# Second tile's gated outputs in the normed input's place, and the last queries' transposes tied into the second gate projection

## The chip, the cores and the metric

The kernel runs on one core of one Trainium2 chip. The metric is the device time of one execution in microseconds. Three runs of the kernel before gave 296.37 us as the median (296.13 to 296.43). A core has a matrix engine (PE, with its weight loads as PEld), three engines for element-wise work (DVE, ACT, POOL) and a sync engine (SP) that issues the DMAs. PE writes only to PSUM, which has eight banks; DVE and ACT read them out.

## What is computed

Two layers on 256 tokens of width 1024, in float32. Each layer is `x = x + rms_norm(mixer(rms_norm(x)))`. Layer 0's mixer is gated linear attention and isn't touched. Layer 1's is sparse attention with 16 heads in 4 groups:

```python
p = (h @ w_in)                       # queries, six key/value parts, gate logits, gate path z
q = rope(q, positions) * DH ** -0.5
...                                  # compressed, selected and windowed attention, per group
o = einsum('bshc,bshcd->bshd', gates, out).reshape(B, S, NSA_Q) * silu(z)
return o @ w_out
```

## The kernel before

The 256 tokens are two tiles t of 128. Every large product is made of three float32r matmuls (high by high, high by low, low by high half: `mm3`, L211 to L213), so each weight and each activation is split: ACT makes the high half (L190), DVE or POOL the low one (L196).

The stretch that the change touches begins once layer 1's keys and values are there. Its parts, in the order in which the program names them (L1209 to L1235):

- Query projections Q(p, t) for half p of the heads and tile t (`q_steps`). Each ends with the rotary embedding: two DVE products and a POOL sum (L827), which leaves the rotated queries in `qr`.
- Query transposes QT(p, t) (`q_T`): four PE transposes (L982) into one PSUM bank of the tag "t", then two ACT copies (L987) and two DVE subtractions (L988) into a tile of the tag "qS".
- Gate projections Z0 and Z1 (`z_steps`): 96 matmuls each, eight steps k of twelve, which read the normed input `hT` and fill the two "acc" banks. At the end DVE and ACT make the gate `zT` from them (L362, L372, L373).
- Units U(g, t), one for each group g and tile t. `scores` makes four heads of scores (L1020) in the three "s" banks; DVE masks them and takes the minimum (L1025), ACT takes the exponential (L1027), POOL weighs the result (L1061). `values` transposes the weighed scores into "t" banks, four transposes a round (L1091), copies each round out by ACT or DVE in turn (L1095, L1097), and multiplies with the values (L1105); one transpose for the compressed part (L1111) and the products of it (L1129) end it. A unit of tile 0 has two rounds, one of tile 1 four. There are two "t" banks.
- `finish` multiplies a unit's output with the gate (L356) and splits it (L357, L358) into `ofT[t]`, the gated outputs. These are four tiles (two tokens' tiles, high and low) of the tag "qS", which has six buffers that hold the queries too.
- Output projections O0 and O1 (`out_steps`): 48 matmuls each, into the "acc" banks.

So the order is: Q(0,1), U(0,0), QT(0,1), Z0, U(1,0), Q(1,0), the gated outputs of U(0,0) and U(1,0), QT(1,0), Q(1,1), U(2,0), QT(1,1), Z1, U(3,0), their gated outputs, the loads and splits of the output weights, O0, the four units of tile 1, O1.

A planner turns this into one fixed queue for each engine: among the instructions that are ready by its estimated times it takes the one named first. What it may pass is limited by `chain`, which holds the projections' matmuls among themselves in program order, by `after` (behind a given instruction in the queue, without a semaphore), and by `paced`: the splits of the output weights are tied to steps of Z1 (L1230; 2 of 8 halves of the first 512 columns and 2 of 8 of the second to steps 2 and 3, the others to steps 4 to 7). The raw weights have four buffers.

Of the kernel before, what the change touches and what calls it, by code (L numbers as in the profile page):

```python
# [10 lines left out]
F32R = mybir.dt.float32r  # L11
# [5 lines left out]
P = 128  # L17
D = 1024
S = 256
NT = S // P  # L20
KT = D // P
# [66 lines left out]
def hybrid_kernel(ctx: ExitStack, tc: tile.TileContext, x, positions, pre_norm, post_norm,  # L88
# [3 lines left out]
    nc = tc.nc  # L92
    base = ctx.enter_context(tc.tile_pool(name="base", bufs=1))
# [4 lines left out]
    def nm(s):  # L98
        _n[0] += 1
        return f"{s}_{_n[0]}"  # L100

    def bank(tag="t"):
        return ps.tile([P, 512], F32, tag=tag, name=nm(tag), bufs=BANKS[tag])

    def f(ap):
        return ap.bitcast(F32)

    def after(ins, prev):

        if prev is not None:  # L110
            tc.add_manual_dep(ins.ins, prev.ins.name, mybir.DependencyInfo(
                mybir.DependencyClass.NoSync, mybir.DependencyReason.DATA), reason="issue order")
        return ins
# [10 lines left out]
    def dma(dst, src):  # L124
        queue[0] = after(nc.sync.dma_start(dst, src), queue[0])
# [5 lines left out]
    lp = l1.enter_context(tc.tile_pool(name="l1", bufs=1))  # L131
    C1 = lp.tile([P, C_L1 - C_L0], F32, tag="c1", name="c1")

    def cc(name):
        o, w = COFF[name]
        t, at = (C0, 0) if o < C_L0 else (C1, C_L0) if o < C_L1 else (C2, C_L1)
        return t[:, o - at:o - at + w]
# [10 lines left out]
    ident = cc("ident")  # L148
# [61 lines left out]
    def mm3(o, a, b, start, stop, **kw):  # L210
        m = nc.tensor.matmul(o, a[0], b[0], start=start, stop=False, **kw)  # L211
        nc.tensor.matmul(o, a[0], b[1], start=False, stop=False, **kw)  # L212
        return m, nc.tensor.matmul(o, a[1], b[0], start=False, stop=stop, **kw)  # L213
# [3 lines left out]
    def chain(first, final):  # L217

        after(first, last[0])
        last[0] = final  # L220
# [42 lines left out]
    def residual(t, o, gb):  # L263

        ss = base.tile([P, 8], F32, tag="ss", name=nm("ss"), bufs=4)
        yg = [base.tile([P, H], F32, tag="xg", name=nm("yg"), bufs=2) for _ in range(2)]

        def done(n):
            nc.scalar.activation(yg[n], o[n], AF.Square, accum_out=ss[:, n:n + 1])  # L269
            if n == 0:  # L270
                nc.vector.tensor_scalar(ss[:, 2:3], ss[:, 0:1], D * EPS, None, op0=ALU.add)
            else:

                nc.vector.tensor_add(ss[:, 4:5], ss[:, 1:2], ss[:, 2:3])
                nc.gpsimd.tensor_tensor(ss[:, 3:4], ss[:, 4:5], half[:, :1], op=ALU.pow)
            nc.vector.scalar_tensor_tensor(yg[n], o[n], float(D ** 0.5), gb[:, n * H:(n + 1) * H], op0=ALU.mult,  # L276
                                           op1=ALU.mult)
            if n == 1:
                for m in range(2):
                    xx = X[:, t, m * H:(m + 1) * H]  # L280
                    nc.vector.scalar_tensor_tensor(xx, yg[m], ss[:, 3:4], xx, op0=ALU.mult, op1=ALU.add)
        return done
# [77 lines left out]
    def gate_of(o, dst):  # L360

        nc.vector.tensor_tensor(dst, o.rearrange("p (j n) -> p j n", j=2), rb.unsqueeze(1).to_broadcast([P, 2, S]),  # L362
                                op=ALU.mult)
        th = base.tile([P, 2, S], F32, tag="xg", name=nm("th"), bufs=2)
        silu2(dst, dst, th)
# [196 lines left out]
    w, n = wraw[:RANK + 1], RANK + 1  # L562
# [24 lines left out]
    b = bank()  # L587
# [44 lines left out]
    for t in range(NT):  # L632
# [3 lines left out]
        for hp in range(2):  # L636
            b = bank()
# [7 lines left out]
        if t == 0:  # L645
            b = bank()
# [17 lines left out]
        b = bank()  # L664
# [21 lines left out]
    ch_z = [Chunk(w_in, G_Z, 512).load(homes=homes)]  # L686
# [7 lines left out]
    for t in range(NT):  # L694
        aT = aTs[t]
        ob = []
        for hp in range(2):
            b = bank("s")
            for hh in range(2):
                h = 2 * hp + hh  # L700
# [5 lines left out]
        if t == 0:  # L706
            Ssb = [lp.tile([P, GH, GDV], F32R, tag=a, name=nm("S")) for a in ("q", "k")]
            for hp in range(2):
                b = bank("s")
                for hh in range(2):  # L710
                    h = 2 * hp + hh
# [15 lines left out]
    for c in range(2):  # L727
# [4 lines left out]
        for t in range(NT):  # L732
            b = bank()
# [52 lines left out]
    lp = ctx.enter_context(tc.tile_pool(name="l2", bufs=1))  # L786
# [106 lines left out]
    ch_z = [Chunk(w_in, N_Z + p * 512, 512) for p in range(2)]  # L893
# [43 lines left out]
    def pe(m):  # L937
        return m

    def run(steps, n=99):  # L940
        for _ in range(n):
            if next(steps, None) is None:
                break
# [8 lines left out]
                done(o)  # L952
            yield 1

    def proj_T_steps(chunk, done):
        o = [bank("acc") for _ in range(2)]
        for k in range(KT):
            for j in range(4):
                a, b = mm3(o[j // 2][:, (j % 2) * S:(j % 2 + 1) * S], chunk.part(k, j * P, (j + 1) * P),
                           [h[:, k, :] for h in hT], k == 0 and j % 2 == 0, k == KT - 1, skip_group_check=True)  # L960
                chunk.mm.setdefault(2 * k, a)
                chunk.mm[2 * k + 1] = a
                chain(a, b)
            if k == KT - 1:
                done(o)
            yield 1

    qS, qr = {}, {}

    def q_steps(p, t):  # L970

# [5 lines left out]
    def q_T(p, t):  # L977

        b = bank()
        r = qr[p, t]  # L980
        for m in range(4):
            pe(nc.tensor.transpose(b[:, m * P:(m + 1) * P], r[:, 2 * m:2 * m + 2].rearrange("p h d -> p (h d)"), ident))  # L982
        q = lp.tile([P, 2, 4, P], F32R, tag="qS", name=nm("qS"), bufs=6)
        bv = b.rearrange("p (m n) -> p m n", m=4)
        h = (slice(0, 64), slice(64, 128))
        for a in range(2):
            nc.scalar.activation(q[h[a], a], bv[h[a]], AF.Copy)  # L987
            nc.vector.tensor_sub(q[h[1 - a], a], bv[h[a]], f(q[h[a], a]))  # L988
        qS[p, t] = q

    def z_steps(p):
        def done(o):
            for j in range(2):
                gate_of(o[j], zT[:, p * 4 + j * 2:p * 4 + j * 2 + 2, :])
        return proj_T_steps(ch_z[p], done)

    def small(n, tag):
        return ap_.tile([P, n], F32, tag=tag, name=nm(tag), bufs=2)
# [150 lines left out]
    def out_steps(t, before=None):  # L1149

        o = [bank("acc") for _ in range(2)]
        steps = [(k, n) for k in range(6) for n in range(2)] + [(k, n) for n in range(2) for k in range(6, KT)]
        done = residual(t, o, gpost)
        for k, n in steps:
            a, b = mm3(o[n], [h[:, k, :] for h in ofT[t]], ch_o[n].part(k), k == 0, k == KT - 1)
            if before and (k, n) == (LATE, 0):
                after(a, before())
            chain(a, b)
            if k == KT - 1:
                done(n)  # L1160
            yield 1
        for n in range(2):
            sl = slice(n * H, n * H + H)
            dma(out[0, t * P:(t + 1) * P, sl], X[:, t, sl])
# [7 lines left out]
    b = bank()  # L1172
# [8 lines left out]
    b = bank()  # L1181
# [9 lines left out]
    for p in range(2):  # L1191
        for G in range(2):
# [3 lines left out]
                                    cc("blk")[rows].unsqueeze(2).to_broadcast([64, 4, DH]), op=ALU.mult)  # L1196
    run(q00)
    q_T(0, 0)
    l2a.close()
    ap_ = ctx.enter_context(tc.tile_pool(name="l2b", bufs=1))  # L1200
    ofT = [[lp.tile([P, KT, P], F32R, tag="qS", name=nm("ofT"), bufs=6) for n in "hl"] for t in range(NT)]
    ch_o = [Chunk(nsa_w_out[0], c * 512, 512) for c in range(2)]
    U = {(g, t): Unit(g, t) for g in range(GROUPS) for t in range(NT)}

    def unit(g, t):
        run(U[g, t].scores())
        run(U[g, t].values())

    ch_z[0].load().split((ch_q[0], 8))  # L1209
    run(q_steps(0, 1))  # L1210
    unit(0, 0)
    q_T(0, 1)
    run(z_steps(0))
    ch_q[1].load().split((ch_z[0], 0))
    unit(1, 0)
    run(q_steps(1, 0))
    for g in range(2):
        U[g, 0].finish()
    q_T(1, 0)
    ch_z[1].load().split((ch_q[1], 0))  # L1220
    run(q_steps(1, 1))
    unit(2, 0)
    q_T(1, 1)
    run(z_steps(1))
    unit(3, 0)
    for g in range(2, 4):
        U[g, 0].finish()
    for k in (0, 2, 4, 6):
        for n in range(2):
            ch_o[n].load(k, k + 2).split((ch_z[1], k + 2 * n + PA[12]))  # L1230
    run(out_steps(0))
    for g in range(GROUPS):
        unit(g, 1)
        U[g, 1].finish()
# [31 lines left out]
```

## Time and profile before

| what | value |
|---|---|
| median of three runs | 296.37 us (296.13 to 296.43) |
| the profiled execution | 296.34 us |
| its span, first to last instruction | 294.3 us |
| busy: PE, PEld, DVE, ACT, POOL | 281.9, 238.1, 203.9, 178.5, 178.7 us |
| mean granted TensorE clock | 0.993 |

What lies between the span and the execution's time is 296.34 - 294.3 = 2.04 us. A busy time is the sum over an engine's instructions; PE's matmuls overlap, so their busy time hides waits, and their starts tell more. The chain of waits follows the last instruction back to what released it. In the timeline a row is start, length, engine, line, operation, result and operand, count, and in square brackets an idle time before it with what ended it.

### The profile page before, as it was taken

How to read it: one execution, taken by the hardware profiler on the slowest of the kernel's cores; microseconds unless marked ns; L12 is line 12 of the kernel's file. 1: busy time of each engine (PE TensorE's matmuls, PEld its weight loads, DVE VectorE, ACT ScalarE, POOL GpSimd, SP SyncE). 2: the span in 40 equal slices, each digit the busy share in tenths (PEclk: the TensorE clock that was granted, in tenths of full speed). 3: DMA queues.
4: the chain of work that ended last, by engine and by line, in shares of the span. 5: the costliest groups of instructions: out<-in, count | busy, mean ns of one | idle time of the engine just before them, and what ended most of it. 6: DMA issues, size and time to landing. Idle time of an engine off the chain costs nothing.

```text
span 294.3 us, 5427 instructions
## 1 busy us (share of the span) xinstructions
PE 281.9 (96%) x1836; PEld 238.1 (81%) x1836; DVE 203.9 (69%) x515; ACT 178.5 (61%) x464; POOL 178.7 (61%) x207
## 2 busy tenths in 40 slices
PE   8999999999999999889999999999999899999991
PEld 7888999999999887668898789986889667678560
DVE  1779668854989968577469668797539976585323
ACT  4896788676665665545427436486278797565311
POOL 1496968985376033823539194569799779366400
PEclk9999999999999999999999999999999999999997
DMA  7997589114667255189897475704353000010001
GB/s 213 403 399 208 146 247 292 39 67 145 213 206 224 74 145 143 28 198 358 266 377 220 145 209 155 211 1 155 132 149 136 4 0 2 0 72 2 0 0 71
DMA packets 28300, 44.56 MB, mean 151 GB/s; under 512 B 2865, under 2 KB 12513, under 8 KB 28274
## 3 DMA queue, kind: packets, MB, share of 16 engines
q1 hardware_dynamic: 28242, 44.23, 47.7%
q8 instruction: 14, 0.23, 0.3%
q14 instruction: 12, 0.10, 0.1%
q10 hardware_dynamic: 32, 0.01, 0.0%
HBM read 43.18 MB, written 1.05 MB: 150 GB/s over the span
## 4 chain that ended last, share of the span: by engine, by line
PE 75%; DVE 8%; issue 7%; POOL 4%; ACT 3%; DMA 1%; SPq 0%; DVEq 0%; POOLq 0%; ACTq 0%
PE acc L213 13%; PE acc L212 13%; PE acc L211 13%; PE s L211 4%; PE s L212 4%; PE s L213 4%; PE s L468 4%; PE o L1105 4%; PE s L1020 3%; PE t L1091 3%; PE o L904 2%; DVE lo L196 2%; DMA raw<-in_gla_w_in_dram 1%; PE o L1129 1%; POOL lo L196 1%
## 5 line engine op out<-in xcount | busy, mean ns | idle before, releaser
L196 POOL TENSOR_TENSOR lo<-raw,hi 128x512 fp32r<-128x512 f32 (+2 forms) x63 | 83.6, 1350 | 41.8 <-ACT hi L190 41.8
L190 ACT ACTIVATE hi<-raw 128x512 fp32r<-128x512 f32 (+2 forms) x120 | 62.7, 581 | 17.7 <-DMA raw<-in_nsa_w_in_dram 6.1
L196 DVE TENSOR_TENSOR lo<-raw,hi 128x512 fp32r<-128x512 f32 (+2 forms) x57 | 56.1, 1006 | 11.2 <-ACT hi L190 11.0
L212 PE MATMUL acc<-hT,hi 128*128 128x256 f32 x160 | 45.0, 282 | 0.0
L211 PE MATMUL acc<-hT,hi 128*128 128x256 f32 x160 | 45.0, 281 | 0.0
L213 PE MATMUL acc<-hT,lo 128*128 128x256 f32 x160 | 44.5, 281 | 0.0
L1061 POOL TENSOR_SCALAR P<-P,cf,gates 128x128 f32<-128x128 f32 (+1 forms) x64 | 33.9, 545 | 14.2 <-DVE cf L1057 9.2
L213 PE MATMUL acc<-hi,hT 128*128 128x512 f32 (+2 forms) x104 | 36.0, 346 | 0.8 <-DVE hT L311 0.8
L211 PE MATMUL acc<-hi,hT 128*128 128x512 f32 (+2 forms) x104 | 35.8, 345 | 0.8 <-DVE yg L276 0.7
L212 PE MATMUL acc<-lo,hT 128*128 128x512 f32 (+2 forms) x104 | 35.5, 341 | 0.0
L1027 ACT ACTIVATE P<-P,mn 128x128 f32<-128x128 f32 (+1 forms) x64 | 28.4, 445 | 9.3 <-DVE mn L1025 8.9
L212 PEld LDWEIGHTS acc<-hT,hi 128*128 128x128 f32 x160 | 30.1, 188 | 0.3
L211 PEld LDWEIGHTS acc<-hT,hi 128*128 128x128 f32 x160 | 30.0, 188 | 0.1
L213 PEld LDWEIGHTS acc<-hT,lo 128*128 128x128 f32 x160 | 29.8, 188 | 0.0
L1025 DVE CUSTOM_DVE_ANT_0 P<-s,c 128x128 f32<-128x128 f32 (+1 forms) x64 | 20.8, 350 | 5.7 <-PE s L1020 3.5
L211 PEld LDWEIGHTS acc<-hi,hT 128*128 128x128 f32 x104 | 19.6, 188 | 3.7 <-ACT yg L269 1.2
L213 PEld LDWEIGHTS acc<-hi,hT 128*128 128x128 f32 x104 | 19.6, 188 | 3.3 <-DVE hT L311 1.7
L212 PEld LDWEIGHTS acc<-lo,hT 128*128 128x128 f32 x104 | 19.6, 188 | 1.8
L1091 PE MATMUL t<-c,P 128*128 128x128 f32 x96 | 17.6, 287 | 0.7 <-POOL P L1061 0.3
L440 POOL TENSOR_TENSOR lo<-raw,hi 128x512 fp32r<-128x512 f32 (+1 forms) x9 | 12.3, 1388 | 9.7 <-ACT hi L436 9.6
L1091 PEld LDWEIGHTS t<-c,P 128*128 128x128 f32 x96 | 10.8, 140 | 6.6 <-issue 3.1
L1020 PE MATMUL s<-kTh,qS 128*128 128x272 f32 (+1 forms) x48 | 14.5, 316 | 0.1
(271 smaller groups left out, 668.1 us busy)
## 6 DMA issues: line engine op xcount, KB each, us to landing
raw<-in_nsa_w_in_dram SPq DMA_DIRECT2D x24, 512.0 KB, 4.4
raw<-in_gla_w_in_dram SPq DMA_DIRECT2D x12, 512.0 KB, 5.5
raw<-in_gla_w_out_dram SPq DMA_DIRECT2D x8, 512.0 KB, 4.3
raw<-in_nsa_w_out_dram SPq DMA_DIRECT2D x8, 512.0 KB, 4.2
raw<-in_nsa_w_in_dram SPq DMA_DIRECT2D x8, 280.0 KB, 6.1
raw<-in_gla_w_in_dram SPq DMA_DIRECT2D x6, 344.0 KB, 3.4
home<-in_gla_w_in_dram SPq DMA_DIRECT2D x4, 512.0 KB, 6.7
w<-in_nsa_ck_w_dram SPq DMA_DIRECT2D x4, 512.0 KB, 7.4
```

Source lines behind the costliest of these rows:

```text
L190: m = after(nc.scalar.activation(hi[:, j, :n], raw[:, j, :n], AF.Copy), prev)
L196: eng.tensor_sub(lo[:, j, :n], raw[:, j, :n], f(hi[:, j, :n]))
L211: m = nc.tensor.matmul(o, a[0], b[0], start=start, stop=False, **kw)
L212: nc.tensor.matmul(o, a[0], b[1], start=False, stop=False, **kw)
L213: return m, nc.tensor.matmul(o, a[1], b[0], start=False, stop=stop, **kw)
L440: line(e, eng.tensor_sub(lo[:, j, :n], raw[:, j, :n], f(hi[:, j, :n])))
L468: m = nc.tensor.matmul(o[t][:, :chunk.n], hT[i][:, k, t * P:(t + 1) * P], w[j], start=(k == b == 0), stop=(k == KT - 1 and b == 2))
L1020: pe(nc.tensor.matmul(o, q[i], k[:, g, c0:c1], start=(m == 0), stop=(m == 1)))
L1025: nc.vector.tensor_tensor_reduce(out=o, in0=src, in1=masks[br], op0=ALU.add, op1=ALU.min, scale=-0.125, scalar=3.0e38, accum_out=self.mn[: ...
L1027: nc.scalar.activation(o, o, AF.Exp, scale=-1.0, bias=self.mn[:, j:j + 1], accum_out=self.sm[:, j:j + 1])
L1061: nc.gpsimd.tensor_scalar(o, o, cf[:, i * 2 + br:i * 2 + br + 1], gates[:, t, 4 * g + 2 * h + i, br + 1:br + 2], op0=ALU.mult, op1=ALU.mult)
L1091: pe(nc.tensor.transpose(b[:, i * P:(i + 1) * P], self.Pt[i][:, c0:c0 + P], ident))
```

## The change

The gated outputs of tile 1 get a place of their own: one tile of the tag "hTh", the buffer of the normed input's high half, cut in two for the high and low halves. It is named after O0, and the input is last read by Z1. The gated outputs of tile 0 stay among the "qS" buffers. And Z1 gets two ties: its first matmul of step 1 stands behind the last transpose of QT(1,0), that of step 4 behind the last of QT(1,1).

```diff
-    def proj_T_steps(chunk, done):
+    def proj_T_steps(chunk, done, behind={}):
...
                 chunk.mm[2 * k + 1] = a
+                if j == 0:
+                    after(a, behind.get(k))
                 chain(a, b)
...
-    qS, qr = {}, {}
+    qS, qr, qt = {}, {}, {}
...
-            pe(nc.tensor.transpose(b[:, m * P:(m + 1) * P], r[:, 2 * m:2 * m + 2].rearrange("p h d -> p (h d)"), ident))
+            qt[p, t] = nc.tensor.transpose(b[:, m * P:(m + 1) * P], r[:, 2 * m:2 * m + 2].rearrange("p h d -> p (h d)"),
+                                           ident)
...
-    def z_steps(p):
+    def z_steps(p, behind={}):
...
-        return proj_T_steps(ch_z[p], done)
+        return proj_T_steps(ch_z[p], done, behind)
...
-    ofT = [[lp.tile([P, KT, P], F32R, tag="qS", name=nm("ofT"), bufs=6) for n in "hl"] for t in range(NT)]
+
+    ofT = [[lp.tile([P, KT, P], F32R, tag="qS", name=nm("ofT"), bufs=6) for n in "hl"]]
...
-    run(z_steps(1))
+
+    run(z_steps(1, {1: qt[1, 0], 4: qt[1, 1]}))
...
     run(out_steps(0))
+    both_of = base.tile([P, KT, S], F32R, tag="hTh", name="ofT1")
+    ofT.append([both_of[:, :, :P], both_of[:, :, P:]])
```

## Rows read from the trace of the kernel before

**Rows 1.** The chain of waits, shares of the span by engine.
```profile
PE 75%; DVE 8%; issue 7%; POOL 4%; ACT 3%; DMA 1%; SPq 0%; DVEq 0%; POOLq 0%; ACTq 0%
```
**Rows 2.** Windows: stretch, length, busy (count) of PE, PEld, DVE, ACT, POOL; clock, DMA.
```profile
218.00:223.70 5.70, 5.70 (x51) 5.70 (x50) 4.53 (x6) 4.78 (x10) 5.70 (x6) 1.00 0.86 263
223.70:230.30 6.60, 6.60 (x36) 5.57 (x35) 6.60 (x26) 5.83 (x22) 4.95 (x4) 1.00 0.03 11
230.30:245.60 15.30, 13.72 (x91) 9.72 (x90) 13.03 (x78) 13.31 (x51) 12.60 (x30) 1.00 0.01 2
245.60:262.40 16.80, 16.54 (x105) 11.79 (x104) 11.21 (x47) 10.31 (x35) 10.71 (x19) 1.00 0.08 32
...
288.10:294.30 6.20, 0.00 (x0) 0.00 (x0) 2.31 (x5) 0.69 (x2) 0.55 (x1) 0.66 0.22 85
```
**Rows 3.** PE by form, 230.3 to 245.6 us: count, busy, mean ns, idle before.
```profile
L1020 PE MATMUL s<-kTh,qS 128*128 128x272 f32 (+1 forms) x18 | 5.8, 334 | 0.1
L1091 PE MATMUL t<-c,P 128*128 128x128 f32 x24 | 5.4, 300 | 0.6 <-POOL P L1061 0.3
...
L1129 PE MATMUL o<-pcT,vblk 64*128 64x128 f32 x8 | 1.4, 297 | 0.0
L1105 PE MATMUL o<-pT,vs_sb 128*64 128x256 f32 x8 | 1.3, 404 | 0.6 <-ACT pT L1095 0.6
```
**Rows 4.** The chain of waits after 240 us: start, length, what, count.
```profile
255.80 0.58 PE o L1105 x4
...
256.97 0.64 PE o L1129 x4
257.61 0.59 PE t L1091 x4
258.19 0.73 PE s L1020 x6
```
**Rows 5.** Timeline of POOL: the rotary sum of Q(1,1), and low halves of weights.
```profile
210.36 1.29 POOL L827 TENSOR_TENSOR rt<-rt,rt 128x512 f32<-128x512 f32 x1 [1.69 <-PE t L1091]
211.61 7.99 POOL L196 TENSOR_TENSOR lo<-raw,hi 128x512 fp32r<-128x512 f32 x6
```
**Rows 6.** Timeline of PE: query transposes, Z1's first and last matmul, U(2,0)'s first.
```profile
202.02 0.66 PE L982 MATMUL t<-c,rt 128*128 128x128 f32 x4
...
208.66 0.28 PE L211 MATMUL acc<-hT,hi 128*128 128x256 f32 x1
...
214.33 0.66 PE L982 MATMUL t<-c,rt 128*128 128x128 f32 x4
...
222.84 0.29 PE L1020 MATMUL s<-kTh,qS 128*128 128x272 f32 x1
...
223.57 0.28 PE L213 MATMUL acc<-hT,lo 128*128 128x256 f32 x1
...
236.86 0.60 PE L982 MATMUL t<-c,rt 128*128 128x128 f32 x4
```
**Rows 7.** Timeline of DVE: a gate product, a round's copy, and last query subtractions.
```profile
194.47 0.82 DVE L373 SCALAR_TENSOR_TENSOR zT<-th,zT 128x512 f32<-128x512 f32 x1
...
196.40 0.67 DVE L1097 COPY pT<-t 128x512 f32<-128x512 f32 x1
...
205.58 0.69 DVE L988 TENSOR_TENSOR qS<-t,qS 64x512 fp32r<-64x512 f32 x1 [0.45 <-ACT qS L987]
...
222.03 0.69 DVE L988 TENSOR_TENSOR qS<-t,qS 64x512 fp32r<-64x512 f32 x1
```
**Rows 8.** Timeline of ACT: a round's copy in U(2,0), and U(0,1)'s first gated output.
```profile
234.73 0.60 ACT L1095 ACTIVATE pT<-t 128x512 f32<-128x512 f32 x1
...
260.45 0.40 ACT L357 ACTIVATE ofT<-of 128x256 fp32r<-128x256 f32 x1
```
**Rows 9.** Timeline of PE before 190 us: U(0,0)'s first score matmul.
```profile
186.25 0.29 PE L1020 MATMUL s<-kTh,qS 128*128 128x272 f32 x1
```
**Rows 10.** Timeline of SP's queue: loads of the output weights.
```profile
198.40 22.18 SPq L125 DMA_DIRECT2D raw<-in_nsa_w_out_dram  x8
```

## The prediction

> **What bounds the kernel now.** I read the chain of waits first: three quarters of the span are PE [rows 1]. So the time is PE's work plus its waits, and a change that only moves work is worth what it does to the waits. Second, the windows. From 218.0 to 223.7 us PE runs Z1 almost alone, 51 matmuls in 5.70 us, 0.112 us each: no wait. From 223.7 to 230.3 it lives on the first half of O0, while DVE is busy for all of its 6.60 us. From 230.3 to 245.6 it has 91 matmuls in 15.30 us and two engines beside it nearly full (DVE 13.03, ACT 13.31); from 245.6 to 262.4 105 matmuls fill 16.80 us [rows 2].
>
> Third, what PE has to do in 230.3 to 245.6, by form: 18 pairs of score matmuls, 24 round transposes, 8 matmuls of L1129, 8 of L1105 (and 8 more on the window's values), and some 7 small ones [rows 3]. The chain prices them: six score matmuls 0.73, four transposes 0.59, four of L1129 0.64, four of L1105 0.58 [rows 4]. That is 36 x 0.122 + 24 x 0.148 + 2 x 0.64 + 4 x 0.58 + about 1.3 = 4.4 + 3.5 + 1.3 + 2.3 + 1.3 = 12.8, against 15.3. So PE waits about 2.5 us here; with transposes at 0.11, what a Z1 matmul takes, it is 3.4. I use 3.0. The reason stands in the timeline: Z1 is spent by 223.57, U(2,0)'s first score comes at 222.84 [rows 6], and the rest of O0 needs the outputs of U(2,0) and U(3,0). PE has nothing to fill with.
>
> **The change part by part.** *Place of tile 1's outputs.* No instruction is added or removed; the copies and subtractions write as many elements. What is new is that they wait for Z1's last read of the input. The first comes at 260.45 [rows 8], Z1 ends at 223.57 [rows 6]: 37 us of cover, of which the rest of the change uses at most some 15. What goes is the need for two of six "qS" buffers; the queries' tile of QT(1,1) then can't be held up by them. It can gain nothing by itself, since its transposes need only a bank, and it loses nothing. 0.
>
> *Z1's step 1 behind QT(1,0).* Today Z1 starts at 208.66 and QT(1,0) stands at 214.33, among Z1's steps [rows 6]. Now only twelve Z1 matmuls may stand before it. From 208.66: 12 x 0.112 = 1.3, six round transposes of U(1,0) 0.9, its two products 1.2, the compressed transpose 0.15, QT itself 0.6: it ends at 212.8 instead of 214.99. PE doesn't stand still, since what is queued ahead is ready; the gain is that the copies of QT(1,0) can start 2.2 us sooner, and the splits tied to steps 2 and 3 no longer stand before them.
>
> *Z1's step 4 behind QT(1,1).* This is the part that decides. Q(1,1) is rotated by 210.36 + 1.29 = 211.65 [rows 5], but its transposes come at 236.86 [rows 6], 25 us later, past a whole Z1 that is named after them. They need only a bank. U(2,0)'s rounds are named before, and one is copied out from 234.73 to 235.33 [rows 8]; QT(1,1) follows. I read this as: the two banks go out in the program's order, so QT(1,1) can't pass U(2,0)'s rounds. The diff doesn't change that order. Then the tie doesn't pull QT(1,1) forward, it holds Z1's steps 4 to 7, 48 x 0.112 = 5.4 us of work, until U(2,0)'s rounds are copied out. Behind them on PE wait O0 (by the chain of projections), and by the pace of Z1 twelve of the sixteen halves of the output weights: their ACT copies, DVE and POOL subtractions, and the loads that wait for the raw buffers, which SP issued until 220.58 before [rows 10].
>
> How long is Z1 held? Copying queries out took 4.2 us after 202.02 (the last subtraction ends at 205.58 + 0.69) and 8.4 us after 214.33 (it ends at 222.72) [rows 6, 7]. I take 4.2, the case without splits and gated outputs in front. From first score to last round copied out took 10.8 us in U(0,0) (186.25 to 196.40 + 0.67) and 12.5 us in U(2,0) (222.84 to 235.33) [rows 6 to 9]. In U(0,0) a gate projection's four DVE products (two like the 0.82 at 194.47, two of about 0.7) stood before that copy; with Z1 held there are none, so I take 8.0. Then QT(1,1) stands at 212.8 + 4.2 + 8.0 = 225.0.
>
> In these 12.2 us PE can do: Z1's steps 1 to 3 (36 x 0.112 = 4.0), U(1,0)'s last products 0.64, the scores of U(2,0) and U(3,0) (16 x 0.122 = 2.0), nine transposes 1.3, U(2,0)'s two products 1.2, half of the scores of U(0,1) 1.0: 10.1. A hole of 2.1 us opens. In return Z1's 5.4 us and then all of O0 lie where PE waits now, and the 3.0 us there go. Sum: 2.1 - 3.0 = -0.9 us, a span of 293.4 against 294.3. With the 2.04 us around it, 295.4 against the profiled 296.34, which stands 0.03 below the median.
>
> Bounds: copying out can't be under 2.6 us (two ACT copies and two subtractions in turn, 0.6 and 0.69), which makes the hole 0.5 and the sum -2.5, -2.9 with 3.4 us of waits. With 8.4 and 12.5 it is 20.9 us of hold against 11.7 us of work (all of U(0,1)'s scores, U(2,0)'s L1129), a hole of 9.2 and a sum of +6.2.
>
> *A rule that speaks against it.* In the window with the waits the granted clock is 1.00, full 2.4 GHz; it fell to 0.66 on average only in the last 6.20 us, in which PE has no matmul at all [rows 2]. The Trainium skill ("TensorE: Matmul & The Clock Gate", "Why this matters for your kernels") warns that a TensorE left idle between bursts falls back to half its clock. By that rule a hole in one piece would make the held half of Z1 run at 1.2 GHz. The trace agrees only for the end; waits spread among score matmuls left the clock alone here, and the hole would be of that kind.
>
> **Rivals.** *1. The hole is longer than the waits (slower).* Place: PE between the end of Z1's step 3 and QT(1,1). It decides from QT(1,1) later than 225.9, 0.9 us after my estimate. For it: no row has a unit of 8.0 us. With the shortest rows as they are (4.2 and 10.8) the hold is 15.0, the work 10.6, the hole 4.4, the sum +1.4: 297.7; with the longest 302.5. Against it: with Z1 held, fewer splits and no gate products crowd U(2,0).
>
> *2. The waits come back (no change).* The held splits fall on POOL together with the weighing of U(3,0) and U(0,1). Six low halves took 7.99 us [rows 5]; eight or nine after 225 are 11 us, in a stretch where POOL is busy for 12.60 of 15.30 [rows 2]. Then U(0,1)'s rounds come no earlier than now and about 0.9 us of waits stays: 296.3. Against it: POOL is free of those halves before.
>
> *3. The tie holds nothing.* If the banks don't go out in order, QT(1,1) stands near 214 as its operands allow, no hole opens, and all that is left is QT(1,0)'s 2.2 us: 294.1. Against it: the 25 us above.
>
> *4. The clock falls in the hole.* 48 matmuls at half speed cost 5.4 more: 300.8. Against it: the 1.00 above.
>
> **How the numbers follow.** My forecast 0.43, with its own range 293.4 to 295.8; rival 1 0.33, rival 2 0.17, rival 3 0.05, rival 4 0.02. What this kernel's runs can tell from no change is about 0.2%, 0.6 us. Faster: the forecast and most of rival 3, 0.47. Same: rival 2 and the edge of rival 3, 0.18. Slower: rivals 1 and 4, 0.35. The range goes down to the lower bound (-2.9, 293.4) and a little under it for waits after 245.6 that I haven't priced, 293.0; upward through most of rival 1, to 299.6.
>
> **What would show it.** QT(1,0) within twelve Z1 matmuls of Z1's start, ending near 212.8. U(2,0)'s first score near 217, not 222.84. A gap or thin stretch on PE of about 2 us before QT(1,1), and QT(1,1) near 225, right behind U(2,0)'s rounds. Z1's end after 231. O0 in one piece, without the waits of 230 to 245. Tile 1's first gated output without a wait for the input. I am wrong if QT(1,1) stands ahead of U(2,0)'s rounds; if it stands after 226 the sign turns; and if POOL ends every wait between 228 and 245, rival 2 holds.

## The result: 306.6 us, 3.4% slower

The changed kernel takes 306.59 us (median of 4 runs, 305.89 to 307.11), the kernel before 296.40 beside it. The ratio is 1.0343, with a 95% interval of 1.032 to 1.0365. The forecast was 295.4, the range up to 299.6: wrong, and on the other side. The profiled execution has a span of 304.2 us against 294.3, so 9.9 us have to be found in the rows.

The chain of waits answers to [rows 1]. PE's share fell from 75% of 294.3 (221 us) to 71% of 304.2 (216 us): what was added to the chain is not PE's.

```profile
PE 71%; DVE 9%; issue 8%; POOL 4%; ACT 4%; DMA 2%; SPq 0%; DVEq 0%; POOLq 0%; ACTq 0%
```

The windows of the changed kernel, columns as in [rows 2], and two short stretches taken out of them:

```profile
218.00:223.70 5.70, 3.87 (x21) 2.67 (x20) 4.60 (x39) 4.33 (x20) 1.72 (x5) 1.00 0.43 149
223.70:230.30 6.60, 4.52 (x28) 2.87 (x26) 4.20 (x30) 6.58 (x29) 6.60 (x18) 0.93 0.01 2
230.30:245.60 15.30, 13.10 (x79) 11.77 (x78) 14.00 (x19) 7.90 (x17) 9.75 (x12) 0.83 0.22 70
245.60:262.40 16.80, 16.80 (x93) 12.51 (x92) 10.75 (x41) 9.79 (x34) 11.51 (x20) 0.97 0.00 1
...
229.50:232.50 3.00, 2.68 (x13) 2.68 (x14) 1.01 (x4) 3.00 (x8) 3.00 (x9) 0.50 0.02 5
243.50:246.00 2.50, 2.50 (x8) 1.92 (x7) 2.50 (x9) 2.50 (x7) 0.67 (x1) 0.50 0.00 0
```

Two readings. First, idle time: from 218.0 to 245.6 PE is idle for 1.83 + 2.08 + 2.20 = 6.1 us, where it was idle for 1.6 before [rows 2]: 4.5 more. Second, the clock column: before, it is 1.00 in every stage until the last matmul; now it falls to 0.50, 1.2 GHz, twice. Length times missing clock is 6.60 x 0.07 + 15.30 x 0.17 + 16.80 x 0.03 = 3.6 us. Together that is an estimated 8.1 of the 9.9 us. Part of the rest are the first matmuls after each wait, which take longer (0.36 to 0.39 us against 0.28); I didn't sum them.

The timeline of PE shows where (the number in brackets is the idle time before the row, and what ended it). Lines stand two or three further down than in the kernel before: L984, L991, L1023 and L1094 here are its L982, L988, L1020 and L1091.

```profile
212.41 0.66 PE L984 MATMUL t<-c,rt 128*128 128x128 f32 x4
...
217.91 0.39 PE L1023 MATMUL s<-kTh,qS 128*128 128x272 f32 x1
...
219.83 0.39 PE L1023 MATMUL s<-kTh,qS 128*128 128x272 f32 x1 [1.41 <-DVE qS L991]
...
228.18 0.65 PE L1108 MATMUL o<-pT,vs_sb 128*64 128x256 f32 x4 [0.94 <-ACT pT L1098]
...
229.82 0.42 PE L1114 MATMUL t<-c,cS 128*64 128x128 f32 x1 [0.55 <-POOL cS L1080]
230.03 1.06 PE L984 MATMUL t<-c,rt 128*128 128x128 f32 x4
230.75 0.56 PE L211 MATMUL acc<-hT,hi 128*128 128x256 f32 x1
231.11 0.41 PE L212 MATMUL acc<-hT,hi 128*128 128x256 f32 x1
231.32 0.41 PE L213 MATMUL acc<-hT,lo 128*128 128x256 f32 x1
...
238.15 0.28 PE L213 MATMUL acc<-hT,lo 128*128 128x256 f32 x1
...
241.81 0.63 PE L1094 MATMUL t<-c,P 128*128 128x128 f32 x4 [2.20 <-DVE qS L991]
242.44 0.50 PE L211 MATMUL acc<-hi,ofT 128*128 128x512 f32 x1
...
243.78 0.63 PE L212 MATMUL acc<-lo,ofT 128*128 128x512 f32 x1
244.21 0.63 PE L213 MATMUL acc<-hi,ofT 128*128 128x512 f32 x1
```

QT(1,0) is at 212.41 and QT(1,1) at 230.03, right behind U(2,0)'s rounds and its compressed transpose (L1114): 17.6 us apart, and Z1's step 4 waits for it. Z1's first matmuls after it come 0.21 us apart, where they took 0.112, and it ends at 238.15, not 223.57 [rows 6]. Then PE stands still for 2.2 us, and O0's matmuls come 0.43 apart.

What ended those 2.2 us is seen on DVE and POOL:

```profile
219.09 0.69 DVE L991 TENSOR_TENSOR qS<-t,qS 64x512 fp32r<-64x512 f32 x1
...
231.82 0.68 DVE L991 TENSOR_TENSOR qS<-t,qS 64x512 fp32r<-64x512 f32 x1 [1.21 <-ACT qS L990]
232.54 8.39 DVE L196 TENSOR_TENSOR lo<-raw,hi 128x512 fp32r<-128x512 f32 x2
240.97 0.69 DVE L991 TENSOR_TENSOR qS<-t,qS 64x512 fp32r<-64x512 f32 x1
```

```profile
222.40 5.23 POOL L1064 TENSOR_SCALAR P<-P,cf,gates 128x128 f32<-128x128 f32 x12 [3.98 <-DVE cf L1060]
...
227.78 1.73 POOL L1064 TENSOR_SCALAR P<-P,cf,gates 128x128 f32<-128x128 f32 x4
229.48 0.29 POOL L1080 TENSOR_TENSOR cS<-cS,cs 128x64 f32<-128x64 f32 x1
...
232.28 7.50 POOL L196 TENSOR_TENSOR lo<-raw,hi 128x512 fp32r<-128x512 f32 x6
```

Two subtractions of output weights took DVE 8.39 us, where one alone takes 0.69, while POOL ran six of the same kind back to back. Behind them in DVE's queue stood the second subtraction of QT(1,1)'s queries (240.97), which frees the bank that U(3,0)'s second round waits for. Grouped by line, L196 on DVE has a median of 840 ns and one row of 7793 (minimum, median, maximum):

```profile
L196 DVE TENSOR_TENSOR lo<-raw,hi x57: 431/840/7793, 33.0 to 248.8; 128x512 fp32r<-128x512 f32 x44, 128x280 fp32r<-128x280 f32 x9, 128x344 fp32r<-128x344 f32 x4
```

The Trainium skill ("SBUF — State Buffer", "SBUF: two separate sides") says that a DVE operation with two inputs in SBUF and a GpSimd (POOL) operation that reads SBUF exclude each other for a whole instruction. The trace agrees that DVE is shut out, but over six instructions of POOL, not one: the row of 7793 ns starts at 232.54 and ends 0.55 us behind the six, which end at 239.78.

### The profile page after: what moved, and what is told of

It is laid out like the page before. It is cut to its first block, busy times and chain, and to the rows that moved or that the text cites. A ratio compares the mean times of both kernels' runs of the same rounds, so it can differ in the third digit from the quotient of the medians.

```text
span 304.2 us, 5424 instructions
## 1 busy us (share of the span) xinstructions
PE 286.2 (94%) x1836; PEld 241.6 (79%) x1836; DVE 209.4 (69%) x515; ACT 178.2 (59%) x464; POOL 176.3 (58%) x207
## 4 chain that ended last, share of the span: by engine, by line
PE 71%; DVE 9%; issue 8%; POOL 4%; ACT 4%; DMA 2%; SPq 0%; DVEq 0%; POOLq 0%; ACTq 0%
PE acc L211 13%; PE acc L213 13%; PE acc L212 13%; PE s L211 4%; PE s L212 4%; PE s L213 4%; DVE lo L196 4%; PE s L468 4%; PE o L1108 3%; PE s L1023 3%; PE o L904 2%; PE t L1094 2%; DMA raw<-in_gla_w_in_dram 2%; DVE P L1028 1%; ACT P L1030 1%
## 5 line engine op out<-in xcount | busy, mean ns | idle before, releaser
L196 POOL TENSOR_TENSOR lo<-raw,hi 128x512 fp32r<-128x512 f32 (+2 forms) x63 | 83.0, 1339 | 48.6 <-ACT hi L190 48.6
L196 DVE TENSOR_TENSOR lo<-raw,hi 128x512 fp32r<-128x512 f32 (+2 forms) x57 | 61.7, 1106 | 11.2 <-ACT hi L190 11.1
L1064 POOL TENSOR_SCALAR P<-P,cf,gates 128x128 f32<-128x128 f32 (+1 forms) x64 | 32.6, 522 | 17.7 <-DVE cf L1060 17.3
L212 PEld LDWEIGHTS acc<-hT,hi 128*128 128x128 f32 x160 | 30.5, 191 | 0.3
L211 PEld LDWEIGHTS acc<-hT,hi 128*128 128x128 f32 x160 | 30.6, 191 | 0.2
L1094 PE MATMUL t<-c,P 128*128 128x128 f32 x96 | 17.2, 281 | 2.4 <-DVE qS L991 2.2
L1023 PE MATMUL s<-kTh,qS 128*128 128x272 f32 (+1 forms) x48 | 15.4, 332 | 2.3 <-DVE qS L991 1.4
L1094 PEld LDWEIGHTS t<-c,P 128*128 128x128 f32 x96 | 11.2, 140 | 6.6 <-issue 4.3
```

The source lines that it names most:

```text
L196: eng.tensor_sub(lo[:, j, :n], raw[:, j, :n], f(hi[:, j, :n]))
L1023: pe(nc.tensor.matmul(o, q[i], k[:, g, c0:c1], start=(m == 0), stop=(m == 1)))
L1064: nc.gpsimd.tensor_scalar(o, o, cf[:, i * 2 + br:i * 2 + br + 1], gates[:, t, 4 * g + 2 * h + i, br + 1:br + 2], op0=ALU.mult, op1=ALU.mult)
L1094: pe(nc.tensor.transpose(b[:, i * P:(i + 1) * P], self.Pt[i][:, c0:c0 + P], ident))
```

## The experiments

Every trace starts at its own zero: at the same early instruction (QT(0,0)) they are up to 1.4 us apart, so I compare distances within a trace. Medians of the kernel before beside these runs are 296.9 to 297.1; beside the changed kernel it was 296.4, so a difference to the changed kernel's 306.59 carries some 0.5 us. I write A for the theory that the hold of Z1's step 4 behind QT(1,1), through the order of the banks, is what costs the time.

**e1_place.** Both ties out, the place of tile 1's outputs kept.

```
-    run(z_steps(1, {1: qt[1, 0], 4: qt[1, 1]}))
+    run(z_steps(1, {}))
```

> The change without both ties: only the place of the second tile's outputs is new. Theory A (Z1's step 4, held behind QT(1,1), which can't pass U(2,0)'s rounds, costs the time): as before, 296.4 within 0.6, since Z1's last read of the input ends some 37 us ahead of the first write. Theory B (the place costs or gives time): over 300, with a wait of ACT or DVE ahead of the first gated copy of U(0,1).

296.81 us, ratio 0.9998 (0.9985 to 1.001). The place is worth nothing; all of the loss is the ties.

**e2_tie1** and **e3_tie4.** One tie each: `{1: qt[1, 0]}` and `{4: qt[1, 1]}`.

> The change with the tie of step 1 (behind QT(1,0)) alone. Theory A: no hole; QT(1,0) still ends near 212.8 us, Z1 runs through and ends before 226; the time 294.5 to 296.8. Theory C (either tie alone holds Z1 long enough to upset what follows): over 299.

> The change with the tie of step 4 (behind QT(1,1)) alone. Theory A: nearly all of the loss stands here, 304 to 308, with QT(1,1) behind 228 us and a thin stretch on PE ahead of it. Theory C: the loss is shared, 299 to 303.

The tie of step 1 alone: 300.79 us, 1.0126 (1.0099 to 1.0152), a miss for A. The tie of step 4 alone: 309.09 us, 1.0422 (1.0395 to 1.0448), more than both together and above the range of either theory. So step 4's tie is the costly one, but step 1's isn't free. In e2_tie1 Z1 runs through without a hole; what is different is one wait ahead of U(2,0)'s compressed transpose, and the clock behind it. Its wait and its window:

```profile
239.16 0.30 PE L1114 MATMUL t<-c,cS 128*64 128x128 f32 x1 [1.66 <-POOL cS L1080]
```

```profile
230.30:245.60 15.30, 13.12 (x65) 9.23 (x63) 10.71 (x50) 10.93 (x41) 11.37 (x25) 0.81 0.00 0
240.00:246.00 6.00, 6.00 (x26) 4.45 (x26) 3.95 (x13) 4.01 (x11) 1.67 (x4) 0.50 0.00 0
```

In e3_tie4 the clock is at 0.63 from 223.7 to 230.3 and back at 1.00 behind it, and the wait at the second place is 3.58 us, behind one DVE subtraction of 7.66:

```profile
223.70:230.30 6.60, 6.11 (x28) 5.41 (x27) 6.51 (x53) 6.58 (x33) 5.24 (x12) 0.63 0.01 2
230.30:245.60 15.30, 10.55 (x81) 9.23 (x82) 12.04 (x14) 8.06 (x22) 12.22 (x19) 1.00 0.19 57
```

```profile
244.54 0.63 PE L1094 MATMUL t<-c,P 128*128 128x128 f32 x4 [3.58 <-DVE qS L991]
```

**e4_early**, **e5_early_notie**, **e12_early_before.** QT(1,1) is named ahead of U(2,0): with the whole change; without the ties; and in the kernel before.

```
-    unit(2, 0)
-    q_T(1, 1)
+    q_T(1, 1)
+    unit(2, 0)
```

> The whole change, but QT(1,1) is named ahead of U(2,0), so that it gets its bank ahead of U(2,0)'s rounds. Theory A (the order in which the banks are given out is what makes the hold): QT(1,1) stands before 220 us, no hole ahead of Z1's step 4, the granted clock stays at 1.00 there, and the time is 294 to 297. Rival (the hold comes from the rotation or the ties themselves): QT(1,1) still behind 225, time over 302.

> The place of the second tile's outputs and QT(1,1) named ahead of U(2,0), without either tie. If the ties are idle once the banks go out in that order: 296 to 297, as with both ties. If the tie of step 1 still costs or gives something: more than 0.6 us from 296.5.

> The kernel before with QT(1,1) named ahead of U(2,0) and nothing else: no ties, the second tile's outputs where they were. If the order of the banks is all that matters: QT(1,1) before 220 and 295 to 297, the same as with the ties. Rival (the ties or the place add something once the order is right): over 297.2.

296.49 us, 0.9982 (0.9968 to 0.9996); 296.47, 0.9976 (0.9959 to 0.9992); 296.67, 0.9991 (0.9976 to 1.0007). In e4_early QT(1,1) stands 2.9 us behind QT(1,0) (213.43), Z1 isn't held, and the clock stays up:

```profile
216.36 0.66 PE L984 MATMUL t<-c,rt 128*128 128x128 f32 x4
```

```profile
218.00:223.70 5.70, 5.70 (x51) 5.70 (x50) 4.34 (x10) 5.60 (x12) 5.70 (x6) 1.00 0.57 187
223.70:230.30 6.60, 6.39 (x39) 5.44 (x37) 6.51 (x25) 5.38 (x19) 6.60 (x5) 1.00 0.46 153
230.30:245.60 15.30, 14.40 (x91) 10.25 (x90) 13.45 (x77) 13.10 (x54) 13.24 (x30) 1.00 0.00 1
```

One moved line takes the 10 us away with both ties in place: A holds for the cause. (The line moves QT(1,1) in PE's queue as well as among the banks. Its operands weren't what it waited for: in the changed kernel they were there from 211.82, 18 us ahead.) Mended, the ties have nothing left to do, and the gain over the kernel before is 0.2%, at the edge of what can be told; these three kernels can't be told from each other.

**e8_unheld.** None of the output weights' splits waits for Z1's later steps.

```
-            ch_o[n].load(k, k + 2).split((ch_z[1], k + 2 * n + PA[12]))
+            ch_o[n].load(k, k + 2).split((ch_z[1], k + 2 * n + PA[12] - 12))
```

> The whole change, but the output weights' splits are paced twelve half steps earlier, so that none of them waits for a step of Z1 after its third. Theory A (the hole ahead of QT(1,1) is most of the loss): QT(1,1) still near 230, the 2.2 us wait at 241.8 goes, time 302 to 305. Theory C (the held splits are most of the loss): QT(1,1) before 226 and time 296 to 300.

308.37 us, 1.0396 (1.0335 to 1.0457): a miss for both. The splits, brought forward, stand in front of U(1,0)'s and QT(1,0)'s copies; PE waits there instead, and the clock falls three times:

```profile
216.03 0.42 PE L1114 MATMUL t<-c,cS 128*64 128x128 f32 x1 [1.34 <-POOL cS L1080]
...
226.10 0.59 PE L1023 MATMUL s<-kTh,qS 128*128 128x272 f32 x1 [2.27 <-DVE qS L991]
```

It moved the collision, and says nothing on the price of the held splits.

**e9_alldve** and its control **e15_before_alldve.** POOL makes none of the sixteen low halves of the output weights, in the changed kernel and in the kernel before.

```
-LOS = (..., (0, 1, 2, 3, 4, 5, 6, 7), (1, 2, 5))
+LOS = (..., (), ())
```

> The whole change, but POOL makes none of the output weights' low halves; DVE makes all sixteen, 16 x 0.68 = 10.9 us. If DVE's one subtraction of 7.79 us is long because POOL runs six beside it: no weight subtraction on DVE over 1.9 us, the wait ahead of U(3,0)'s second round under 0.8 us in place of 2.2, time 303 to 306. Rival (it is long for another reason, its input or its queue): a row of several us stays, and time 306 or more.

> Control: the kernel before with the output weights' sixteen low halves all on DVE and none on POOL. If the 6 us that this division gave back in the changed kernel come from POOL's six subtractions shutting DVE out there: no such gain here, 295.5 to 299. Rival (POOL's share of these halves is a bad division everywhere): 290 to 294.

Changed: 300.31 us, 1.012 (1.0096 to 1.0144), 6.3 us back, more than either theory gave. Before: 298.49, 1.0064 (1.004 to 1.0088), 1.6 us worse. So the division is no better in itself; in the changed kernel it takes the shut-out away. L196 on DVE in e9_alldve:

```profile
L196 DVE TENSOR_TENSOR lo<-raw,hi x68: 428/690/1801, 33.1 to 242.3; 128x512 fp32r<-128x512 f32 x55, 128x280 fp32r<-128x280 f32 x9, 128x344 fp32r<-128x344 f32 x4
```

The wait of 2.2 us and the second stretch of half clock are gone with it; the hole and, in the profiled run, the first stretch are as in the changed kernel (clock 0.90 in 230.3 to 245.6). Two of the four runs kept a mean clock of 0.997, where the profiled one has 0.987, and took 299.69 and 299.91 us against its 300.71. **e16_early_alldve**, the same division on e4_early, was the last try at a faster version.

> QT(1,1) named ahead of U(2,0) with both ties, and all sixteen low halves on DVE. If DVE's waits beside POOL are on the path there (rows of 1.46, 1.65 and 1.78 us): 294 to 296. If DVE is the fuller engine in that stretch (13.45 of 15.30 us): 297 to 300.

298.82 us, 1.0072 (1.0049 to 1.0094): in the range of the second. PE waits there for DVE (1.13, 0.62 and 0.85 us). And PE works for only 4.00 of 6.60 us, less than in the changed kernel (4.52), but the clock stays at 1.00:

```profile
223.70:230.30 6.60, 4.00 (x24) 3.04 (x24) 6.49 (x21) 4.75 (x12) 0.00 (x0) 1.00 0.37 104
```

**e13_fillz.** 38 matmuls of zeros (`zz`), added into Z1's accumulators in the hole, behind U(2,0)'s four scores and two rounds (`marks`).

```
+            if k == 4 and behind:
+                for m, x in enumerate(marks[2, 0]):
+                    for i in range((5, 5, 5, 5, 9, 9)[m]):
+                        y = nc.tensor.matmul(o[0][:, :S], zz, hT[1][:, 0, :], start=False, stop=False, skip_group_check=True)
+                        after(y, x)
```

> The whole change, with 38 matmuls of a tile of zeros (128x256, some 0.118 us each, 4.5 us in all) added to Z1's accumulators between its steps 3 and 4, tied to the scores and rounds of U(2,0), so that they lie in the hole. The output is unchanged. Theory D (the thin use of PE brings the granted clock down, and that is part of the price): the half-clock stretch of 229.4 to 232.8 goes, QT(1,1) is within 1 us of 230.0, time 304 to 306. Rival (the clock falls whatever PE does there): the stretch stays, and time is 306.6 to 309.

301.34 us, 1.0153 (1.0138 to 1.0168): 5.3 us back by adding 4.5 us of work, more than theory D gave. QT(1,1) stands 17.1 us behind QT(1,0) (230.11 and 213.04), so the hold is nearly as long, and the clock doesn't fall:

```profile
223.70:230.30 6.60, 6.54 (x51) 5.31 (x50) 5.49 (x38) 6.54 (x29) 6.33 (x17) 1.00 0.02 5
230.30:245.60 15.30, 15.30 (x103) 12.87 (x102) 12.70 (x23) 10.59 (x25) 13.80 (x15) 1.00 0.23 70
```

More came back than the first stretch cost (229.4 to 232.8 at half speed, 1.7 us). But POOL's queue has another order here: two of the halves stand ahead of the weighing of U(0,1) (230.63), and the six come later (236.55), behind the queries' subtraction. They shut out a gate product instead, for 4.91 us; nobody on PE waited for it. So the 5.3 us aren't the clock's alone:

```profile
239.74 4.91 DVE L373 SCALAR_TENSOR_TENSOR zT<-th,zT 128x512 f32<-128x512 f32 x1
```

```profile
230.63 2.55 POOL L196 TENSOR_TENSOR lo<-raw,hi 128x512 fp32r<-128x512 f32 x2
...
236.55 7.55 POOL L196 TENSOR_TENSOR lo<-raw,hi 128x512 fp32r<-128x512 f32 x6
```

**e19_fillz_alldve.** Both at once.

> The whole change with the 38 matmuls of zeros in the hole and all sixteen low halves on DVE: neither a half clock nor DVE shut out. What is left is the hole. If the three parts add up (hole, half clock in it, DVE shut out with the second half clock): 298.5 to 300.5. If the filling and the division gave back the same 5 to 6 us: 301 to 302.5, no better than either alone.

299.85 us, 1.0094 (1.007 to 1.0117). That is inside the range of the sum, but by the differences it is mostly one loss: 5.3 and 6.3 us apart, 6.7 together. The wait behind the collision at 232 to 241, and the half clock behind that wait, are gone in both: in e9_alldve with POOL's six halves, in e13_fillz with POOL's other order. Z1's return at half speed isn't needed for it: in e3_tie4 Z1 came back at a clock of 1.00, and the subtraction took 7.66 us all the same. And the runs of e9_alldve that kept their clock took 299.69 and 299.91, as long as this kernel: beyond the clock, the zeros add nothing to the division. Left are 2.8 us over the kernel before: zeros that found no gap, the division's own price (1.6 in the control) and the hole. I can't divide these further.

**e14_fillo** and **e18_fill7.** Zeros in the kernel with the tie of step 1 alone: 19 matmuls (4.4 us) over a longer stretch, and 7 (1.6 us) in the one wait. Both add them to O0's first accumulator ahead of its fifth block:

```
+            if t == 0 and (k, n) == (4, 0):
+                for i in range(7):
+                    after(nc.tensor.matmul(o[0], zz, ch_o[0].part(0)[0], start=False, stop=False), marks[2, 0][-1])
```

> The tie of step 1 alone, with 19 matmuls of a tile of zeros (128x512, some 0.233 us each, 4.4 us in all) added to O0's first accumulator between its fourth and fifth block, tied to the rounds of U(2,0) and the scores and first round of U(3,0). The output is unchanged. Theory D (with the tie of step 1 alone nearly all of the 3.7 us lost is the half clock from 239.6 to 246.5): that stretch goes and time is 297 to 299. Rival (the loss is the waits): 300.5 to 303.

> The tie of step 1 alone, with only 7 matmuls of a tile of zeros (128x512, 1.6 us in all), in the place where PE waited 1.66 us for POOL ahead of U(2,0)'s compressed transpose. The output is unchanged. If that wait brings the clock down and the half clock (6.9 us, so up to 3.5 us lost) is the loss of the tie of step 1: no half clock before the last matmul, and 297 to 299. Rival (the loss is in the order that the tie brings, not in the clock): no half clock, and still 300 to 302.

e14_fillo: 301.85 us, 1.0173 (1.0152 to 1.0194), no half clock and no gain. The time is in the rival's range, but the cost of 4.4 us of zeros is in it, so it settles nothing. e18_fill7 mends that: 298.66 us, 1.0071 (1.0045 to 1.0097), 2.1 us back. The zeros and the window:

```profile
237.25 1.89 PE L1162 MATMUL acc<-hi,zz 128*128 128x512 f32 x7
```

```profile
230.30:245.60 15.30, 14.80 (x90) 10.68 (x88) 11.94 (x58) 12.91 (x50) 11.61 (x25) 1.00 0.00 1
```

PE was made to work through a wait that it couldn't avoid, and the program got faster. So the wait brought the clock down, and the clock is some half of what the tie of step 1 lost: 2.1 of 3.7 us by this run (the order of later instructions differs a little too). One of e2_tie1's six runs points the same way: it kept a mean clock of 0.993, where the others have 0.986 or 0.987, and took 299.17 us, 1.6 less than the median. The other 1.6 us of e18_fill7 are not explained.

**e17_alone.** The first scores of U(3,0) and U(0,1) are held behind QT(1,1) too.

```
+                    if (g, t) in ((3, 0), (0, 1)) and i == m == 0:
+                        after(x, qt[1, 1])
```

> The whole change, and the first scores of U(3,0) and U(0,1) also held until QT(1,1) is done, so that U(2,0) has ACT, DVE and POOL to itself. If the units behind it made it last 12.1 us (217.91 to 230.03) in place of the 8.0 of the prediction: QT(1,1) between 224.5 and 227. Rival (a unit needs its 11 to 12 us by itself): QT(1,1) after 228. The time is above 306 by either, since the scores that filled part of the hole are gone, and the clock falls.

303.83 us, 1.0242 (1.0213 to 1.027): QT(1,1) stands after 228, as the rival said; the time is a miss for both. QT(1,1) came 16.2 us behind QT(1,0) (213.59), not 17.6: the units behind it make up little of the hold. From its first score to its last round copied out U(2,0) took 9.05 us by itself (219.09 to 228.14), 10.2 in the changed kernel (217.91 to 228.13). Part of it was at half clock (0.51 from 223.7 to 230.3), so its time at full clock stays open; but its eight transposes, 3.50 us, go at the pace of POOL's eight weighings, 3.51 us:

```profile
219.09 0.39 PE L1023 MATMUL s<-kTh,qS 128*128 128x272 f32 x1
...
223.91 3.50 PE L1096 MATMUL t<-c,P 128*128 128x128 f32 x8 [1.88 <-POOL P L1066]
...
229.80 1.03 PE L984 MATMUL t<-c,rt 128*128 128x128 f32 x4
```

```profile
223.37 3.51 POOL L1066 TENSOR_SCALAR P<-P,cf,gates 128x128 f32<-128x128 f32 x8 [3.76 <-DVE cf L1062]
```

And it is faster than the changed kernel by 2.8 us, against what I expected: with another order behind QT(1,1) its profiled run has no shut-out and no second stretch of half clock.

## Why the prediction was wrong

**Right: the place.** Expected 0, measured 0.9998 (e1_place).

**Right: the mechanism of step 4.** The tie doesn't pull QT(1,1) forward, it holds Z1 until U(2,0)'s rounds are out, and the order in which the two are named is the reason (e4_early). QT(1,0) at 212.41 and U(2,0)'s first score at 217.91 came within 1 us of what was written. The turn was named too: QT(1,1) later than 226 changes the sign.

**Failed: the length of the hold.** This is the step "How long is Z1 held?", 12.2 us; it was 17.6, or 17.0 from QT(1,0)'s end (213.07), where the 12.2 begin. By its terms: copying QT(1,0)'s queries out took 7.4 us (212.41 to 219.09 + 0.69), where I took 4.2, the shorter of two measured values, with the longer at 8.4 [rows 6, 7]. U(2,0) from there until its last round was copied out (228.13) took 8.35, where I took 8.0. That is no proof of the 8.0: U(2,0)'s first score now stands ahead of the last subtraction, and counted from it (217.91), as in the rows, the unit took 10.2, close to the shorter row of 10.8 that I had set aside. Then 1.9 us that I left out: its compressed transpose stands in PE's queue ahead of QT(1,1), and its input comes from POOL at 229.77, behind four weighings of U(3,0) (227.78). The rows of before had 1.5 of them (235.33 to 236.86). Choosing the shorter row for the copies, and less than any row for the unit, was the mistake: the reason given for the copies was that splits and gated outputs no longer stand in front, but the gated outputs of U(0,0) and U(1,0) still did, and so did splits.

```profile
215.90 0.75 ACT L357 ACTIVATE ofT<-of 128x256 fp32r<-128x256 f32 x2 [1.62 <-DVE of L356]
216.56 0.58 ACT L990 ACTIVATE qS<-t 64x512 fp32r<-64x512 f32 x1
...
227.53 0.60 ACT L1098 ACTIVATE pT<-t 128x512 f32<-128x512 f32 x1
```

**Failed: the rivals' prices.** A hold of 17.6 lies between my cases of 15.0 (+1.4) and 20.9 (+6.2), so my own sum would have said about +3.5 us, 300. It was +10.2. Missing were two things. One is the clock, an estimated 3.6 us: rival 4 had the right mechanism and 0.02, because before the change waits among score matmuls left it at 1.00; those waits came to 0.6 us in a group [rows 3]. With single waits of 1.41 and 0.94 in thin work it fell, without a hole in one piece, and not for all 48 matmuls of the rival: for some nine of Z1's, and later for eight of O0's. The rule that I weighed there, from the Trainium skill ("TensorE: Matmul & The Clock Gate", "Why this matters for your kernels"), is borne out in part: the clock did fall to half, but behind short waits in thin work, and in e16_early_alldve such waits left it at 1.00. The other is DVE beside POOL: I wrote that twelve halves are held and land on POOL and DVE together, and priced them by POOL's throughput (rival 2). That six of them, released at once, shut DVE out for 7.8 us, with the queries' subtraction queued behind, was in no case. With it the term of -3.0 us failed, the waits that were to go: from 230.3 to 245.6 PE is idle for 2.20 us, and was for 1.58 before [rows 2].

**Failed: step 1 as a gain.** I put 2.2 us of earlier copies there. Alone that tie costs 3.7 us (e2_tie1), 2.1 of them by one wait and the clock behind it (e18_fill7).

## What to carry to other kernels

A tie that makes filler work wait for something late takes the filler from where it was needed; ask first why the late thing is late. Here one line naming the transposes earlier mends what two ties made worse. When a hold has two measured lengths, price the change at the longer one too, and look at what stands ahead in each engine's queue, up to the last instruction. And price a wait on TensorE twice: its length, and the half clock that can come after it.

## What the runs showed of the hardware

Single waits of 0.9 to 1.7 us on PE, in work that was thin already, were followed by half the clock for several us; in the changed kernel the second stretch costs nearly as much as the wait before it (2.2 us idle, then 8 matmuls of O0 at 0.43 us, where they took 0.23: 1.6). It isn't so each time: e16_early_alldve waited 1.13, 0.62 and 0.85 us within 6.6 us at a clock of 1.00, and two of e9_alldve's four runs kept the clock that its profiled one lost. What decides it was not found. Seven matmuls of zeros in such a wait were worth more than they cost (e18_fill7, 2.1 us); nineteen over a longer stretch weren't (e14_fillo).

DVE can lose to POOL for longer than one instruction. Beside six POOL subtractions in a row one instruction of it lasted 7.79 us (the changed kernel), 7.66 (e3_tie4) and 4.91 (e13_fillz), and ended 0.55 us behind POOL's row each time. In other traces it got in between two of them: in e4_early no DVE subtraction beside a row of seven on POOL took over 1.8 us. What tells the two cases apart was not found.
